# Fewer, larger transfers and a last row stored in seven pieces, in a kernel that scales tokens by their two gate weights

## The chip, the cores and the metric

The kernel runs on one core of a Trainium2 chip. The metric is the device time of one execution in microseconds (us), taken several times; lower is better. Besides the times there is one profiled execution, with the busy spans of every engine, the packets of the DMA engines and what released each wait.

## The reference

Each of 16 x 1024 tokens has 512 float32 values and 8 router logits. The two largest probabilities of a token are scaled so that they sum to 1, and the token is written out twice, once with each weight (the smaller first).

```python
def reference(x, router_logits, k):
    ...
    probs = probs / np.sum(probs, axis=-1, keepdims=True)
    topk_indices = np.argsort(probs, axis=-1)[..., -k:]
    topk_probs = np.take_along_axis(probs, topk_indices, axis=-1)
    topk_probs = topk_probs / np.sum(topk_probs, axis=-1, keepdims=True)
    x_expanded = x[:, :, np.newaxis, :].repeat(k, axis=2)
    return (x_expanded * topk_probs[..., np.newaxis]).astype(np.float32)
```

With k = 2 the weights are the two sigmoids of the difference of the two largest logits. The kernel reads 33.6 MB of x and 0.5 MB of logits and writes 67.1 MB.

## The kernel before

The 16,384 tokens are cut into two groups of 128 x 65 and 128 x 63 (`GROUPS`, L49). Within a group each of the 128 partitions holds 65 (or 63) consecutive tokens, here called rows: "16 rows" is 16 tokens on every partition. A row is 2 KB per partition in x and 4 KB per partition in the output, since each token is written twice. The core's on-chip memory holds one group of x in `xs` (65 rows), which is used again for the second group, and a staging buffer `osp` for 16 output rows.

*Weights.* After the first two loads (L114) both parts of the logits are loaded (L116, L117), and `top2_weights` finds the largest and second largest of 8 for all 128 tokens of a partition in ten small VectorE steps, their difference (L40), and two sigmoids on ScalarE (L42, L43). The result `WA` serves both groups.

*Rows.* A plan says which rows are multiplied in one VectorE instruction (L128) and where the products go; one store follows each (L136). There are two kinds of places: `osp`, and the part of `xs` whose tokens have already been read (`over`, L98 to L104): as 16 input rows become 32 rows' worth of output, a later stretch of rows can be written over earlier ones of `xs`. For each group the plan is: rows 0 and 1 to `osp`; rows 2 to 15 to `osp`; rows 16 to 31 over the first 32 rows of `xs`; rows 32 to 39 and 40 to 47 to the two halves of `osp`; then the rest (`LAST`, L54) over `xs`, in two parts of 9 and 8 rows in group 0 and one of 15 in group 1. Before a place is written again, the store that reads it must have landed: the multiply for rows 32 to 39 waits for the store of rows 2 to 15, and the loads of the second group wait for the stores out of `xs`.

*Queues.* All loads and stores are issued by SyncE, in program order, except the stores of two rows (L135), which are issued by ScalarE. A wait at one SyncE issue holds back everything behind it on SyncE. Group 1's loads stand in program order behind group 0's stores. The 16 DMA engines serve both queues.

Of the kernel before, what the change touches and what calls it, by code (L numbers as in the profile page):

```python
# [1 line left out]

# [4 lines left out]

F32 = mybir.dt.float32
ALU = mybir.AluOpType
ACTF = mybir.ActivationFunctionType  # L10
P = 128


def top2_weights(nc, pool, logits, M, E, tag=""):

    hi, lo, n = None, None, E  # L20
    while n > 1:
        n //= 2
        if hi is None:
            a, b = logits[:, :, 0:n], logits[:, :, n : 2 * n]
            nhi = pool.tile([P, M, n], F32, tag=f"hi{n}{tag}")
            nlo = b
            nc.vector.tensor_tensor(nhi, a, b, op=ALU.max)  # L27
            nc.vector.tensor_tensor(nlo, a, b, op=ALU.min)  # L28
        else:
            a, b = hi[:, :, 0:n], hi[:, :, n : 2 * n]  # L30
            nhi = pool.tile([P, M, n], F32, tag=f"hi{n}{tag}")
            nlo = pool.tile([P, M, n], F32, tag=f"lo{n}{tag}")
            tmp = pool.tile([P, M, n], F32, tag=f"tmp{n}{tag}")
            nc.vector.tensor_tensor(tmp, lo[:, :, 0:n], lo[:, :, n : 2 * n], op=ALU.max)  # L34
            nc.vector.tensor_tensor(nlo, a, b, op=ALU.min)  # L35
            nc.vector.tensor_tensor(nlo, nlo, tmp, op=ALU.max)  # L36
            nc.vector.tensor_tensor(nhi, a, b, op=ALU.max)  # L37
        hi, lo = nhi, nlo
    dlt = pool.tile([P, M], F32, tag=f"dlt{tag}")
    nc.vector.tensor_tensor(dlt, hi[:, :, 0], lo[:, :, 0], op=ALU.subtract)  # L40
    WA = pool.tile([P, M, 2], F32, tag=f"WA{tag}")
    nc.scalar.activation(WA[:, :, 0], dlt, ACTF.Sigmoid, scale=-1.0)  # L42
    nc.scalar.activation(WA[:, :, 1], dlt, ACTF.Sigmoid, scale=1.0)  # L43
    return WA

GROUPS = [65, 63]  # L49

LOADS = [[2, 4, 2, 8, 17, 32], [16, 16, 31]]


LAST = [[(48, 9), (57, 8)], [(48, 15)]]  # L54


@with_exitstack
def kernel(
    ctx: ExitStack,
    tc: tile.TileContext,  # L60
    x: bass.AP,
    router_logits: bass.AP,
    k: bass.AP,
    out: bass.AP,
):
    nc = tc.nc
    B, S, D = x.shape
    E = router_logits.shape[-1]
    N = B * S
    assert int(k) == 2 and E == 8 and N == P * sum(GROUPS)  # L70
    M = N // P

    L = 16
    x_v, o_v, rl_v = [], [], []
    t0 = 0
    for n in GROUPS:
        t1 = t0 + P * n
        x_v.append(
            x.rearrange("b s d -> (b s) d")[t0:t1].rearrange("(p m) d -> p m d", p=P)
        )  # L80
        o_v.append(
            out.rearrange("b s k d -> (b s) k d")[t0:t1].rearrange(
                "(p m) k d -> p m k d", p=P
            )
        )
        rl_v.append(
            router_logits.rearrange("b s e -> (b s) e")[t0:t1].rearrange(
                "(p m) e -> p m e", p=P
            )
        )  # L90
        t0 = t1

    wpool = ctx.enter_context(tc.tile_pool(name="wpool", bufs=1))
    logits = wpool.tile([P, M, E], F32)
    xs = wpool.tile([P, max(GROUPS), D], F32)
    osp = wpool.tile([P, L, 2, D], F32)

    def over(r, n, G):  # L98

        a = 2 * r - G
        return xs[:, a : a + 2 * n, :].rearrange("p (r k) d -> p r k d", k=2)  # L104

    h = L // 2
    e = 2
    m0 = 0
    for g, G in enumerate(GROUPS):
        r = 0  # L110
        for n in LOADS[g]:
            nc.sync.dma_start(xs[:, r : r + n, :], x_v[g][:, r : r + n, :])  # L112
            r += n
            if g == 0 and r == 6:  # L114

                nc.sync.dma_start(logits[:, :G], rl_v[0])  # L116
                nc.sync.dma_start(logits[:, G:], rl_v[1])  # L117
                WA = top2_weights(nc, wpool, logits, M, E)
        assert r == G
        begin = [(0, e, osp[:, :e]), (e, L - e, osp[:, e:])]  # L120
        plan = begin + [
            (L, L, over(L, L, 2 * L)),
            (2 * L, h, osp[:, :h]),
            (2 * L + h, h, osp[:, h:]),
        ]
        plan += [(r, n, over(r, n, G)) for r, n in LAST[g]]
        for r, n, og in plan:
            nc.vector.tensor_tensor(  # L128
                og,
                xs[:, r : r + n, :].unsqueeze(2).to_broadcast([P, n, 2, D]),  # L130
                WA[:, m0 + r : m0 + r + n, :].unsqueeze(3).to_broadcast([P, n, 2, D]),
                op=ALU.mult,
            )

            queue = nc.scalar if n == e else nc.sync  # L135
            queue.dma_start(o_v[g][:, r : r + n], og)  # L136
        m0 += G


# [1 line left out]
_INS = ['x', 'router_logits', 'k']  # L141
_OUTS = [((16, 1024, 2, 512), 'float32')]

_NUMBERS = {'k': 2}


# [26 lines left out]
```

## Time and profile before

| | |
|---|---|
| times of three runs | 241.50, 240.71, 241.03 us (median 241.03) |
| profiled execution, span from first to last instruction | 239.1 us |
| VectorE busy | 142.1 us, 24 instructions |
| of this, multiplies into `osp` (L128) | 69.2 us, 8 instructions |
| of this, multiplies into `xs` (L128) | 69.1 us, 5 instructions |
| ScalarE busy | 1.8 us |
| moved by DMA | 101.19 MB in 3,456 packets |

How to read the profile: "L128" is line 128 of the kernel. `out<-in` names what an instruction writes and reads. "SPq" and "ACTq" are the issuing sides of SyncE and ScalarE, on which a DMA is handed over; q1 is SyncE's DMA queue and q10 ScalarE's. A DMA's "landing" is the moment its last part is reported as arrived. A packet is counted in the stretch of time in which it starts, so in short stretches the shares of the DMA engines can pass 1. The windows view gives, for a stretch of time, the busy time of VectorE, ScalarE and GpSimd with the number of instructions, then the clock, the share of the DMA engines and GB/s.

### The profile page before, as it was taken

The numbers are of one execution on the slowest core, as the hardware profiler recorded it, in microseconds if no ns is written. First come the engines' busy times: TensorE is split into PE (matmuls) and PEld (weight loads), VectorE is DVE, ScalarE is ACT, GpSimd is POOL, SyncE is SP. The second block draws the span as 40 slices with busy tenths as digits, with TensorE's granted clock in tenths as the row PEclk, the third lists the DMA queues.
The fourth block names the chain that finished last, engine by engine and source line by source line (L and its number), as shares of the span: only waits on it lengthen the run. The fifth ranks groups of instructions, "written<-read, shape, count | busy, mean of one in ns | idle before, by whom it ended". The sixth has DMA issues, their size and how long they took to land.

```text
span 239.1 us, 118 instructions
## 1 busy us (share of the span) xinstructions
DVE 142.1 (59%) x24; ACT 1.8 (1%) x3; POOL 0.2 (0%) x4
## 2 busy tenths in 40 slices
DVE  0589999900299699900000699999006999990000
ACT  2000000000000000000000000000000000000000
POOL 0000000000000000000000000000000000000000
DMA  7999989899999999999999999899899898999894
GB/s 254 440 463 426 441 388 526 329 460 460 417 438 406 400 422 438 438 481 396 433 438 438 438 511 396 384 502 394 384 460 515 362 493 367 428 433 486 380 483 175
DMA packets 3456, 101.19 MB, mean 423 GB/s; under 512 B 384, under 2 KB 512, under 8 KB 896
## 3 DMA queue, kind: packets, MB, share of 16 engines
q1 hardware_dynamic: 3168, 99.09, 96.5%
q10 hardware_dynamic: 288, 2.10, 2.1%
HBM read 34.08 MB, written 67.11 MB: 423 GB/s over the span
## 4 chain that ended last, share of the span: by engine, by line
DMA 52%; DVE 33%; issue 4%; SPq 1%; ACT 0%; DVEq 0%
DMA out_dram<-xs 24%; DVE xs L128 18%; DVE osp L128 13%; DMA out_dram<-osp 13%; DMA xs<-in_x_dram 13%; DMA logits<-in_router_logits_dram 3%; SPq L112 0%; DVE nhi L27 0%; DVE logits L28 0%; DVE nlo L36 0%; DVE nhi L37 0%; DVE nlo L35 0%; DVE tmp L34 0%; SPq L116 0%; ACT WA L42 0%
## 5 line engine op out<-in xcount | busy, mean ns | idle before, releaser
L128 DVE TENSOR_TENSOR osp<-xs,WA 128x8192 f32<-128x8192 f32 (+2 forms) x8 | 69.2, 8688 | 62.3 <-DMA xs<-in_x_dram 31.2
L128 DVE TENSOR_TENSOR xs<-xs,WA 128x16384 f32<-128x16384 f32 (+3 forms) x5 | 69.1, 13811 | 2.2 <-DMA out_dram<-xs 2.0
L27 DVE TENSOR_TENSOR nhi<-logits 128x512 f32<-128x512 f32 x1 | 0.7, 691 | 8.5 <-DMA logits<-in_router_logits_dram 8.5
L42 ACT ACT_TABLE_LOAD x1 | 1.3, 1283 | 0.7 <-PEq L154 0.7
L28 DVE TENSOR_TENSOR logits<-logits 128x512 f32<-128x512 f32 x1 | 0.7, 691 | 0.0
L35 DVE TENSOR_TENSOR nlo<-nhi 128x256 f32<-128x256 f32 (+1 forms) x2 | 0.7, 351 | 0.0
L37 DVE TENSOR_TENSOR nhi<-nhi 128x256 f32<-128x256 f32 (+1 forms) x2 | 0.7, 351 | 0.0
L36 DVE TENSOR_TENSOR nlo<-nlo,tmp 128x256 f32<-128x256 f32 (+1 forms) x2 | 0.7, 350 | 0.0
L34 DVE TENSOR_TENSOR tmp<-logits 128x256 f32<-128x256 f32 x1 | 0.4, 417 | 0.0
L42 ACT ACTIVATE WA<-dlt 128x128 f32<-128x128 f32 x1 | 0.3, 315 | 10.4 <-DVE dlt L40 10.4
L40 DVE TENSOR_TENSOR dlt<-nhi,nlo 128x128 f32<-128x128 f32 x1 | 0.3, 291 | 0.0
L43 ACT ACTIVATE WA<-dlt 128x128 f32<-128x128 f32 x1 | 0.3, 298 | 0.0
L34 DVE TENSOR_TENSOR tmp<-nlo 128x128 f32<-128x128 f32 x1 | 0.3, 283 | 0.0
L154 POOL MEMSET const-bfloat16-1.0<- 128x1 bf16 x1 | 0.1, 101 | 0.0
L154 POOL MEMSET const-uint8-127<- 128x1 uint8 x1 | 0.1, 101 | 0.0
L154 POOL MEMSET const-float32-0.0<- 128x1 f32 x1 | 0.1, 98 | 0.2 <-issue 0.2
L154 POOL MEMSET const-float32-1.0<- 128x1 f32 x1 | 0.1, 98 | 0.0
## 6 DMA issues: line engine op xcount, KB each, us to landing
out_dram<-osp SPq DMA_DIRECT2D x4, 4096.0 KB, 20.7
out_dram<-osp SPq DMA_DIRECT2D x2, 7168.0 KB, 32.4
xs<-in_x_dram SPq DMA_DIRECT2D x2, 4096.0 KB, 30.4
xs<-in_x_dram SPq DMA_DIRECT2D x1, 7936.0 KB, 40.9
out_dram<-xs SPq DMA_DIRECT2D x1, 7680.0 KB, 23.1
out_dram<-xs SPq DMA_DIRECT2D x1, 4608.0 KB, 20.4
xs<-in_x_dram SPq DMA_DIRECT2D x1, 4352.0 KB, 22.8
out_dram<-xs SPq DMA_DIRECT2D x1, 4096.0 KB, 21.4
```

Of the source, the lines that this page charges most:

```text
L27: nc.vector.tensor_tensor(nhi, a, b, op=ALU.max)
L28: nc.vector.tensor_tensor(nlo, a, b, op=ALU.min)
L34: nc.vector.tensor_tensor(tmp, lo[:, :, 0:n], lo[:, :, n : 2 * n], op=ALU.max)
L35: nc.vector.tensor_tensor(nlo, a, b, op=ALU.min)
L36: nc.vector.tensor_tensor(nlo, nlo, tmp, op=ALU.max)
L37: nc.vector.tensor_tensor(nhi, a, b, op=ALU.max)
L40: nc.vector.tensor_tensor(dlt, hi[:, :, 0], lo[:, :, 0], op=ALU.subtract)
L42: nc.scalar.activation(WA[:, :, 0], dlt, ACTF.Sigmoid, scale=-1.0)
L43: nc.scalar.activation(WA[:, :, 1], dlt, ACTF.Sigmoid, scale=1.0)
L128: nc.vector.tensor_tensor(og, xs[:, r : r + n, :].unsqueeze(2).to_broadcast([P, n, 2, D]), WA[:, m0 + r : m0 + r + n, :].unsqueeze(3).to_b ...
L154: nc = _bacc.Bacc("TRN2", target_bir_lowering=False, num_devices=1)
```

## The change

The loads of group 0 are cut 6, 28 and 31 rows instead of 2, 4, 2, 8, 17 and 32; the logits are loaded behind the first of them. Group 1's loads stay 16, 16 and 31. The stores stand in a table, `STORES`, as (first row, rows, place): a number is a row of `osp`, `None` is over `xs`. In group 0 they have 2, 15, 16, 16 and 16 rows, in group 1 16, 16, 16 and 15. Only the first has 2 rows (`EARLY`) and goes to ScalarE's queue. `osp` has 18 rows instead of 16; the logits and the intermediate values of `top2_weights` now lie in its last three rows rather than in tiles of their own; the ten VectorE steps and two sigmoids are the same.

The very last row of group 1 (row 62 of each partition) is taken out of the last store, which then has 14 rows, and is stored in seven transfers of 60, 28, 13, 12, 8, 4 and 3 partitions, all issued by SyncE. That makes 17 whole transfers and 7 pieces instead of 24 whole transfers.

```diff
-LOADS = [[2, 4, 2, 8, 17, 32], [16, 16, 31]]
+LOADS = [[6, 28, 31], [16, 16, 31]]
-LAST = [[(48, 9), (57, 8)], [(48, 15)]]
+STORES = [
+    [(0, 2, 0), (2, 15, 2), (17, 16, None), (33, 16, 0), (49, 16, None)],
+    [(0, 16, 0), (16, 16, None), (32, 16, 0), (48, 15, None)],
+]
+EARLY = 2
+
+LAST_ROW = [[], [60, 28, 13, 12, 8, 4, 3]]
+OSP = 18
...
+    logits = osp[:, OSP - 1].rearrange("p k d -> p (k d)").rearrange("p (m e) -> p m e", e=E)
+    scratch = osp[:, OSP - 3 : OSP - 1].rearrange("p r k d -> p (r k d)")
...
         for n in LOADS[g]:
             nc.sync.dma_start(xs[:, r : r + n, :], x_v[g][:, r : r + n, :])
+            if g == 0 and r == 0:
+                nc.sync.dma_start(logits[:, : GROUPS[0]], rl_v[0])
+                nc.sync.dma_start(logits[:, GROUPS[0] :], rl_v[1])
+                top2_weights(nc, scratch, logits, WA)
             r += n
...
+        for r, n, home in STORES[g]:
+            if home is None:
+                a = 2 * r - (r + n)
+                og = xs[:, a : a + 2 * n, :].rearrange("p (r k) d -> p r k d", k=2)
+            else:
+                og = osp[:, home : home + n]
...
-            queue = nc.scalar if n == e else nc.sync
-            queue.dma_start(o_v[g][:, r : r + n], og)
+            queue = nc.scalar if n == EARLY else nc.sync
+            split = LAST_ROW[g] if r + n == G else []
+            whole = n - bool(split)
+            queue.dma_start(o_v[g][:, r : r + whole], og[:, :whole])
+            p0 = 0
+            for np_ in split:
+                queue.dma_start(
+                    o_v[g][p0 : p0 + np_, r + whole : r + n], og[p0 : p0 + np_, whole:]
+                )
+                p0 += np_
```

More of the change, by code (lines that the diff above doesn't have):

```diff
@@ L11, with top2_weights, cut @@
 P = 128
-def top2_weights(nc, pool, logits, M, E, tag=""):
-    hi, lo, n = None, None, E
+E = 8
+D = 512
+GROUPS = [65, 63]
+M = sum(GROUPS)
+LOADS = [[6, 28, 31], [16, 16, 31]]
[6 more added lines that the diff above has]
+OSP = 18
+def top2_weights(nc, scratch, logits, WA):
+    used = [0]
+    def cut(n):
+        a = scratch[:, used[0] : used[0] + M * n].rearrange("p (m n) -> p m n", n=n)
+        used[0] += M * n
+        return a
+    a, b = logits[:, :, 0:4], logits[:, :, 4:8]
+    hi = cut(4)
+    lo = b
+    nc.vector.tensor_tensor(hi, a, b, op=ALU.max)
+    nc.vector.tensor_tensor(lo, a, b, op=ALU.min)
+    n = 4
@@ L21, in top2_weights @@
     while n > 1:
         n //= 2
[L23 to L37, printed above, removed]
@@ L38, in top2_weights @@
-        hi, lo = nhi, nlo
[L39 to L49, printed above, removed]
-LOADS = [[2, 4, 2, 8, 17, 32], [16, 16, 31]]
-LAST = [[(48, 9), (57, 8)], [(48, 15)]]
+        a, b = hi[:, :, 0:n], hi[:, :, n : 2 * n]
@@ new lines, in top2_weights @@
+        nhi, nlo, tmp = cut(n), cut(n), cut(n)
+        nc.vector.tensor_tensor(tmp, lo[:, :, 0:n], lo[:, :, n : 2 * n], op=ALU.max)
+        nc.vector.tensor_tensor(nlo, a, b, op=ALU.min)
+        nc.vector.tensor_tensor(nlo, nlo, tmp, op=ALU.max)
+        nc.vector.tensor_tensor(nhi, a, b, op=ALU.max)
+        hi, lo = nhi, nlo
+    dlt = cut(1)
+    nc.vector.tensor_tensor(dlt, hi, lo, op=ALU.subtract)
+    nc.scalar.activation(WA[:, :, 0], dlt[:, :, 0], ACTF.Sigmoid, scale=-1.0)
+    nc.scalar.activation(WA[:, :, 1], dlt[:, :, 0], ACTF.Sigmoid, scale=1.0)
@@ L66 @@
     nc = tc.nc
[L67 to L73, printed above, removed]
+    N = x.shape[0] * x.shape[1]
+    assert int(k) == 2 and router_logits.shape[-1] == E and x.shape[2] == D
+    assert N == P * M
+    xf = x.rearrange("b s d -> (b s) d")
+    of = out.rearrange("b s k d -> (b s) k d")
+    rf = router_logits.rearrange("b s e -> (b s) e")
     x_v, o_v, rl_v = [], [], []
@@ L77 @@
         t1 = t0 + P * n
[L78 to L90, printed above, removed]
-        t0 = t1
[L93 to L107, printed above, removed]
+        x_v.append(xf[t0:t1].rearrange("(p m) d -> p m d", p=P))
+        o_v.append(of[t0:t1].rearrange("(p m) k d -> p m k d", p=P))
+        rl_v.append(rf[t0:t1].rearrange("(p m) e -> p m e", p=P))
+        t0 = t1
+    pool = ctx.enter_context(tc.tile_pool(name="pool", bufs=1))
+    xs = pool.tile([P, max(GROUPS), D], F32)
+    osp = pool.tile([P, OSP, 2, D], F32)
+    WA = pool.tile([P, M, 2], F32)
+    logits = osp[:, OSP - 1].rearrange("p k d -> p (k d)").rearrange("p (m e) -> p m e", e=E)
+    scratch = osp[:, OSP - 3 : OSP - 1].rearrange("p r k d -> p (r k d)")
     m0 = 0
@@ L112 @@
             nc.sync.dma_start(xs[:, r : r + n, :], x_v[g][:, r : r + n, :])
+            if g == 0 and r == 0:
+                nc.sync.dma_start(logits[:, : GROUPS[0]], rl_v[0])
+                nc.sync.dma_start(logits[:, GROUPS[0] :], rl_v[1])
+                top2_weights(nc, scratch, logits, WA)
             r += n
[L114 to L127, printed above, removed]
+        for r, n, home in STORES[g]:
[4 more added lines that the diff above has]
+                og = osp[:, home : home + n]
             nc.vector.tensor_tensor(
```

## Prediction

> **What bounds the kernel now.** I read the page first: engine shares, the strip of 40 slices, the DMA queues.
>
> ```profile
> span 239.1 us, 118 instructions
> DVE 142.1 (59%) x24; ACT 1.8 (1%) x3; POOL 0.2 (0%) x4
> DMA  7999989899999999999999999899899898999894
> q1 hardware_dynamic: 3168, 99.09, 96.5%
> q10 hardware_dynamic: 288, 2.10, 2.1%
> HBM read 34.08 MB, written 67.11 MB: 423 GB/s over the span
> ```
>
> VectorE works 59% of the span; the two DMA queues together occupy the 16 DMA engines for 98.6% of it, which is 235.7 us. So the bytes set the time, and the change leaves the bytes alone (101.19 MB). Next the windows view, to see whether any slack lies in the middle.
>
> ```profile
> 2.00:2.50 0.50, 0.00 (x0) 0.01 (x1) 0.00 (x0) 1.00 0.50 74
> 50.00:130.00 80.00, 35.74 (x4) 0.00 (x0) 0.00 (x0) 1.00 1.01 435
> 2.00:237.00 235.00, 142.05 (x24) 0.53 (x3) 0.00 (x0) 1.00 1.00 430
> ```
>
> (Columns: stretch, length, busy VectorE, ScalarE, GpSimd, clock, DMA share, GB/s.) From 2 to 237 us the share is 1.00, so there is no hole to close there, although the chain of waits walks through VectorE. The best steady rate is 435 GB/s. At that rate the bytes need 101.19/0.435 = 232.6 us; 239.1 minus 232.6 leaves 6.5 us for the start, transfer overheads, the mixed load and store stretches and the end. Only from these can this change gain.
>
> The end is seen in the DMA view, by counting packets that start in narrow stretches: 236.66 to 237.30, then to 237.95, then to 238.00. Each DMA engine closes a transfer with one tiny record, so a record tells when an engine is through.
>
> ```profile
> DMA packets 15, 0.00 MB, mean 0 GB/s; under 512 B 15, under 2 KB 15, under 8 KB 15
> DMA packets 0, 0.00 MB, mean 0 GB/s; under 512 B 0, under 2 KB 0, under 8 KB 0
> DMA packets 1, 0.00 MB, mean 0 GB/s; under 512 B 1, under 2 KB 1, under 8 KB 1
> ```
>
> Fifteen engines are through by 237.3; one comes 0.7 to 1.3 us behind them and alone sets the end. Taking the fifteen in the middle of their stretch, the mean is (15 x 236.97 + 237.97)/16 = 237.03, so perfect balance is worth 0.94 us.
>
> **The change part by part.** *Fewer transfers.* 24 whole transfers become 17. What one costs is seen in the DMA view over two stretches of equal bytes: 63.1 to 82.4 (one store of 16 rows), 82.4 to 101.75 (two of 8 rows), and, for small packets, 8.0 to 8.55.
>
> ```profile
> q1 hardware_dynamic: 144, 8.39, 100.3%
> q1 hardware_dynamic: 288, 8.39, 100.4%
> q1 hardware_dynamic: 55, 0.23, 99.4%
> ```
>
> 16-row store: 19.30 x 1.003 = 19.36 us per engine; two 8-row stores: 19.35 x 1.004 = 19.43. Splitting costs 0.07 us, overlap of packets taken out about 0.05. Seven fewer: 7 x 0.05 = 0.35 us gained. The seven pieces give some back: a 4 KB packet takes 0.55 x 16 x 0.994/55 = 0.159 us, where 4 KB inside the 64 KB packets take 19.36/8/16 = 0.151; 8 rows x 0.008 = 0.06, plus seven closing records, under 0.1. Net gain 0.2, bounds 0 to 0.4.
>
> *The second early store goes.* The old kernel puts rows 0 and 1 of each group on ScalarE's queue; the new one does so in the first group only (no store of the second has 2 rows). How late the late engine is, before and after that second early store, from the records in 122.36 to 122.85, to 123.20, to 123.24; then 179.87 to 180.50, to 181.15, to 181.20:
>
> ```profile
> DMA packets 30, 0.49 MB, mean 1003 GB/s; under 512 B 15, under 2 KB 15, under 8 KB 15
> DMA packets 0, 0.00 MB, mean 0 GB/s; under 512 B 0, under 2 KB 0, under 8 KB 0
> DMA packets 2, 0.03 MB, mean 819 GB/s; under 512 B 1, under 2 KB 1, under 8 KB 1
> DMA packets 30, 0.98 MB, mean 1560 GB/s; under 512 B 15, under 2 KB 15, under 8 KB 15
> DMA packets 0, 0.00 MB, mean 0 GB/s; under 512 B 0, under 2 KB 0, under 8 KB 0
> DMA packets 2, 0.07 MB, mean 1311 GB/s; under 512 B 1, under 2 KB 1, under 8 KB 1
> ```
>
> Distance from first to last: 123.2 - 122.36 = 0.84 before, 181.15 - 179.87 = 1.28 after, and the same 1.3 at the end. So 0.45 us of lateness came in where two queues interleaved. I take all 0.45 as gained; the lower bound is 0, if the lateness comes from elsewhere.
>
> *The last row.* Until now each engine gets 8 packets of each transfer (144 records = 128 packets + 16 closings). How rows of a 60- or 13-partition piece are shared out no row shows. Pieces of 13, 12, 8, 4 and 3 rows cannot reach all 16 engines, so some engines get fewer than 8 packets and others more. If the late engine gets none, it saves 8 x 0.159 = 1.27 us, and another, given perhaps three more (0.48), sets the end; if it is one of the favoured, it loses 0.48. Together with the previous item the gain cannot pass the 0.94 of perfect balance. I take 0.85 for both, 0.40 of it here, as the sizes fall so steeply that they fit one engine that is left out; range of both -0.48 to 0.94.
>
> The Trainium skill ("DMA: Bandwidth & Descriptors", section "Why a DMA increments its semaphore by 16 and not by 1") says that a transfer uses the largest divisor of its partition count up to 16, on the lowest-numbered engines. By it the sixteen engines would get 11, 11, 11, 10, 9, 9, 9, 9, 8, 8, 8, 8, 7, 6, 4 and 0 rows; no row of this profile numbers the engines.
>
> *Longer waits for the staging buffer.* `osp` now holds 16 rows per refill at rows 33 of group 0 and 32 of group 1, where the old code refilled it in two halves. The multiply must wait for the landing of the store before last, and its own store must be issued before the running one ends.
>
> ```profile
> 30.33 17.23 DVE L128 TENSOR_TENSOR xs<-xs,WA 128x16384 f32<-128x16384 f32 x1
> 47.58 0.34 SPq L136 DMA_DIRECT2D out_dram<-xs  x1
> 64.42 17.29 DVE L128 TENSOR_TENSOR osp<-xs,WA 128x8192 f32<-128x8192 f32 x2 [16.87 <-DMA out_dram<-osp]
> 73.14 8.93 SPq L136 DMA_DIRECT2D out_dram<-osp  x2
> 83.64 0.03 issue
> 83.74 9.77 DVE xs L128
> 0.73 0.86 SPq L112 DMA_DIRECT2D xs<-in_x_dram  x2
> ```
>
> (Timeline and chain; start, length.) Waking takes 0.10 (83.64 to 83.74), the 16-row multiply 17.24, SyncE's turn 0.02: the new store is issued 17.36 us after the landing. The store that runs meanwhile is 16 rows; landings around one lie 83.64 - 64.32 = 19.32 apart, and this landing at 83.64 comes 0.35 behind the late engine's closing record, which the DMA view has between 83.28 and 83.31:
>
> ```profile
> DMA packets 2, 0.03 MB, mean 1092 GB/s; under 512 B 1, under 2 KB 1, under 8 KB 1
> ```
>
> The late engine therefore runs dry 19.32 - 0.35 = 18.97 after the landing, the first ones 0.85 sooner, 18.1. What counts is the delay from issue to first packet. Nearest rows: the first load is issued at 0.73, and the DMA view has 17 packets starting in 1.74 to 2.20, so about 1.0; the other bound is ScalarE's first store, issued at 15.32, with only the other queue's packets until 18.78 and its own from there to 20.40.
>
> ```profile
> DMA packets 17, 0.07 MB, mean 151 GB/s; under 512 B 0, under 2 KB 0, under 8 KB 17
> 15.32 0.38 ACTq L136 DMA_DIRECT2D out_dram<-osp  x1
> q1 hardware_dynamic: 38, 1.32, 88.8%
> q10 hardware_dynamic: 17, 0.14, 20.3%
> ```
>
> That is 3.46 us, but behind packets of another queue already begun. I take 1.0: first packet at 17.36 + 1.0 = 18.36, so the first engines idle 0.26 and the late one not at all. Cost of the end: 0. At 3.46 the two places cost 2 x (3.46 - 1.61) = 3.7 us.
>
> *The start and the issue queue.* Logits now follow one 6-row load instead of 2 + 4: same bytes ahead, one issue less; the ten small VectorE steps stay. But the 15-row multiply waits for a 28-row load. Until that lands 8.9 MB of x, 0.5 of logits and up to 1.05 of early store move: at 435 GB/s, from about 2.3 us on, it lands at 24 to 26.5.
>
> ```profile
> L128 DVE TENSOR_TENSOR xs<-xs,WA 128x15360 f32<-128x15360 f32 x1 | 16.2, 16158 | 0.0
> L128 DVE TENSOR_TENSOR xs<-xs,WA 128x16384 f32<-128x16384 f32 x2 | 34.4, 17224 | 0.1
> SPq L112 <- DMA out_dram<-xs: 19.8, 2, 10.4
> 102.67 21.33 SPq L112 DMA_DIRECT2D xs<-in_x_dram  x3
> 215.19 0.33 SPq L136 DMA_DIRECT2D out_dram<-xs  x1
> ```
>
> With 16.16 us of multiply its store is issued at 40 to 43; all loads and the early store (18.6 MB) keep the engines until 45. Hidden, with 2 us to spare less the 1.0 of issue; without the cover, up to 1 us. The next 16-row multiply ends 17.2 later, at 60, while the 15-row store runs until 63: hidden too. In group 1 the third load still waits on SyncE for the landing of a store over `xs` (now near 122), and everything behind it on SyncE waits with it; two 16-row loads of 9.7 us each are then queued, and the next store is due only near 149. The seven piece issues come after the last multiply, near 213: 7 x 0.33 = 2.3 us of SyncE, hidden under 17 us of the store ahead of them.
>
> *Sum.* 0.2 + 0.45 + 0.40 = 1.05 us. Profiled span 239.1 - 1.05 = 238.05; the median of the runs, 241.03, lies 1.9 above that span, so **240.0 us**.
>
> **The rivals.** *The engines run dry at the two refills* (the slower side). For it: the margin is 18.97 - 18.36 = 0.6 us, where the old code had ten; ScalarE's delay of 3.46. Against: SyncE's ring is a single queue, and 1.0 was seen on it. It decides once the delay passes 1.61 + 1.05/2 = 2.1; at 2.85, midway from that to the far row, the price is 2 x 1.24 = 2.5, so 242.5 us, at most 243.7.
>
> *The pieces are slow.* Every store in this trace spans all 128 partitions, each engine with rows of its own. If engines that read neighbouring partitions hold each other up, a 60-row piece (4 packets an engine) and a 28-row piece (2) go at half pace, 1.27 + 0.64, and in the others up to four packets queue: 4 x 0.64 + 0.48. Against 11 x 0.159 = 1.75 that is 3.2 us more; half of it, as the engines are not in step, gives 240.0 + 1.6 = 241.6. For it: nothing in this trace; against it: nothing either. The Trainium skill ("SBUF — State Buffer", section on the DMA port swizzle) states the rule that speaks for it: partitions 0 to 63 reach only 8 of 16 ports, with 196 GB/s against 328 for all.
>
> *The change does not touch the late engine*: its lateness is not tied to the second queue, and the pieces do not spare it. Then only 0.2 is left: 240.8 us.
>
> **How the numbers follow.** Forecast 50%, dry engines 18%, slow pieces 20%, late engine untouched 12%. A measurement of this kernel can tell about 0.3%, 0.72 us: faster is below 240.31, slower above 241.75. The forecast's own range is 239.3 to 240.6 (0.94 + 0.4 gained, or half the sum lost); some 85% of it is faster, 43%, and 2% from the third rival: 0.45. Slower: 18% and half of the slow pieces: 0.28. The rest, 0.27, is no change. The range takes in the slow pieces and the lower part of the dry engines: 239.2 to 242.3.
>
> **What would show it.** Right: in the last microseconds the closing records of the row stores no longer leave one engine alone behind; the DMA share stays at 1.00 near 83 and 198 us; no early packets of the second queue in group 1; a span near 238. Wrong: slices below full DMA share right after the two 16-row `osp` multiplies (dry engines); 4 KB packets longer than 0.159 us in the last 3 us (slow pieces); one record 0.8 us behind the rest (late engine untouched). A hole near 43 us would mean that the 28-row load is too large.

## The result and the profile after

The changed kernel takes 243.72 us (median of 4 runs, 243.07 to 244.71) against 240.87 us for the kernel before, measured with it: a ratio of 1.0126, 95% interval 1.0089 to 1.0163. It is 2.85 us slower. The forecast was 240.0 us with a range of 239.2 to 242.3.

The page of the changed kernel, the lines that answer to those of before (below `DMA`, the rate in each of the 40 slices):

```profile
span 241.7 us, 108 instructions
DVE 141.8 (59%) x20; ACT 1.8 (1%) x3; POOL 0.2 (0%) x4
DMA  6998999999999989898979999998989898989993
GB/s 263 539 456 347 401 421 485 382 437 488 391 466 401 466 347 521 347 521 347 521 309 434 434 485 399 483 352 369 499 369 499 380 488 358 510 358 477 446 446 106
q1 hardware_dynamic: 2501, 100.14, 97.3%
q10 hardware_dynamic: 144, 1.05, 1.0%
```

VectorE is unchanged and the DMA engines are as busy as before: 98.3% of a span that is 2.6 us longer, for the same bytes. That is 237.6 us of packets per engine where it was 235.7, so some 1.9 of the 2.6 us is time in which packets were under way but took longer; the rest is idle time. The windows view says where (columns as in the prediction):

```profile
118.00:126.00 8.00, 0.00 (x0) 0.00 (x0) 0.00 (x0) 1.00 0.85 319
158.00:166.00 8.00, 8.00 (x1) 0.00 (x0) 0.00 (x0) 1.00 1.01 389
237.40:238.40 1.00, 0.00 (x0) 0.00 (x0) 0.00 (x0) 1.00 0.98 225
238.40:239.40 1.00, 0.00 (x0) 0.00 (x0) 0.00 (x0) 1.00 0.68 213
239.40:240.40 1.00, 0.00 (x0) 0.00 (x0) 0.00 (x0) 1.00 0.23 82
```

The same two stretches in the kernel before:

```profile
118.00:126.00 8.00, 0.00 (x0) 0.00 (x0) 0.00 (x0) 1.00 0.93 401
158.00:166.00 8.00, 8.00 (x1) 0.00 (x0) 0.00 (x0) 1.00 1.11 476
```

Three places, then. Near 120 us the engines turn from group 0's last store to group 1's first load; near 160 us they turn from group 1's last load to its first store. There the changed kernel is slower, though packets are counted whole in the stretch where they start, so a rate over 8 us is only a pointer. And at the end the pieces run at half the steady rate while the engines are 98% busy in the first of the three stretches.

For the turns I count packets instead. A stretch in which exactly the last 16 packets of a transfer start, one on each engine, gives their mean length: the share times the length of the stretch. The changed kernel in 119.75 to 120.40 (64 KB packets of the last store) and 158.75 to 159.75 (62 KB packets of the last load):

```profile
q1 hardware_dynamic: 16, 1.05, 483.2%
q1 hardware_dynamic: 16, 1.02, 323.9%
```

The kernel before at the same two turns, in 121.10 to 122.05 (32 KB) and 160.50 to 161.50 (62 KB):

```profile
q1 hardware_dynamic: 16, 0.52, 127.7%
q1 hardware_dynamic: 16, 1.02, 246.5%
```

After: 4.832 x 0.65 = 3.14 us against 2.42 for a 64 KB packet in the steady stretch, and 3.24 us. Before: 1.277 x 0.95 = 1.21 us, which is half of 2.42, and 2.47. For 62 KB the share of 2.42 is 2.34. So in the changed kernel these last packets are too long by 0.7 us at the first turn and 0.9 at the second, on average over the engines; the kernel before lost nothing at the first turn and 0.1 at the second. Below, such a lengthening is called a stall.

The refill that I expected to be tight, group 0's, is seen in the timeline of the changed kernel, and in its DMA view for 83.000 to 83.385 and 83.385 to 83.600:

```profile
65.30 17.23 DVE L112 TENSOR_TENSOR osp<-xs,WA 128x16384 f32<-128x16384 f32 x1 [5.69 <-DMA out_dram<-osp]
82.55 0.33 SPq L121 DMA_DIRECT2D out_dram<-osp  x1
```

```profile
DMA packets 5, 0.00 MB, mean 0 GB/s; under 512 B 5, under 2 KB 5, under 8 KB 5
DMA packets 14, 0.59 MB, mean 2743 GB/s; under 512 B 5, under 2 KB 5, under 8 KB 5
```

Up to 83.385 only closing records start; then nine first packets of the new store at once. The first packet comes 0.84 us after the issue. Five engines were done by 83.385 and idled, for 0.3 us at most, as worked out. At this place next to nothing was lost. What it led to later was not in the forecast.

Group 1's refill is another matter. In the profile of the changed kernel with its last row left whole (an experiment below), the new store is issued only at 201.20, and the DMA view for 200.10 to 200.90 and 202.02 to 202.20 shows fifteen closing records and one last packet of the running store, then fifteen first packets of the new one, with nothing starting in between:

```profile
201.20 0.33 SPq L121 DMA_DIRECT2D out_dram<-osp  x1
DMA packets 16, 0.07 MB, mean 82 GB/s; under 512 B 15, under 2 KB 15, under 8 KB 15
DMA packets 15, 0.98 MB, mean 5461 GB/s; under 512 B 0, under 2 KB 0, under 8 KB 0
```

So fifteen engines stood dry for more than 1.1 us. The refill had waited for the landing of an earlier store, and the sixteenth engine was a whole packet behind there; it closes the running store at 202.81 and goes straight on. In the changed kernel itself the gap at this place is shorter: thirteen engines close between 200.45 and 200.98, and the next packets start from 200.98 on.

### The profile page after: what moved, and what is told of

Read it like the earlier page. It is cut to its first block, busy times and chain, and to the rows that moved or that the text cites. A ratio compares the mean times of both kernels' runs of the same rounds, so it can differ in the third digit from the quotient of the medians.

```text
span 241.7 us, 108 instructions
## 1 busy us (share of the span) xinstructions
DVE 141.8 (59%) x20; ACT 1.8 (1%) x3; POOL 0.2 (0%) x4
## 3 DMA queue, kind: packets, MB, share of 16 engines
q10 hardware_dynamic: 144, 1.05, 1.0%
## 4 chain that ended last, share of the span: by engine, by line
DMA 46%; DVE 42%; SPq 1%; issue 0%; DVEq 0%
DVE osp L112 28%; DMA xs<-in_x_dram 24%; DMA out_dram<-osp 22%; DVE xs L112 14%; SPq L102 0%; SPq L103 0%; SPq L100 0%; SPq L121 0%; DVEq L112 0%
## 5 line engine op out<-in xcount | busy, mean ns | idle before, releaser
L112 DVE TENSOR_TENSOR osp<-xs,WA 128x16384 f32<-128x16384 f32 (+2 forms) x5 | 70.1, 14026 | 66.3 <-DMA xs<-in_x_dram 45.7
L112 DVE TENSOR_TENSOR xs<-xs,WA 128x16384 f32<-128x16384 f32 (+1 forms) x4 | 67.8, 16958 | 0.1
L45 DVE TENSOR_TENSOR osp<-osp 128x512 f32<-128x512 f32 x1 | 0.7, 693 | 8.0 <-DMA osp<-in_router_logits_dram 8.0
L46 DVE TENSOR_TENSOR osp<-osp 128x512 f32<-128x512 f32 x1 | 0.7, 693 | 0.0
L55 DVE TENSOR_TENSOR osp<-osp 128x256 f32<-128x256 f32 (+1 forms) x2 | 0.7, 354 | 0.0
L54 DVE TENSOR_TENSOR osp<-osp 128x256 f32<-128x256 f32 (+1 forms) x2 | 0.7, 354 | 0.0
L53 DVE TENSOR_TENSOR osp<-osp 128x256 f32<-128x256 f32 (+1 forms) x2 | 0.7, 353 | 0.0
L52 DVE TENSOR_TENSOR osp<-osp 128x256 f32<-128x256 f32 (+1 forms) x2 | 0.7, 353 | 0.0
L59 ACT ACTIVATE WA<-osp 128x128 f32<-128x128 f32 x1 | 0.3, 316 | 9.9 <-DVE osp L58 9.9
L60 ACT ACTIVATE WA<-osp 128x128 f32<-128x128 f32 x1 | 0.3, 300 | 0.0
```

What stands on the lines that cost most here:

```text
L45: nc.vector.tensor_tensor(hi, a, b, op=ALU.max)
L46: nc.vector.tensor_tensor(lo, a, b, op=ALU.min)
L59: nc.scalar.activation(WA[:, :, 0], dlt[:, :, 0], ACTF.Sigmoid, scale=-1.0)
L60: nc.scalar.activation(WA[:, :, 1], dlt[:, :, 0], ACTF.Sigmoid, scale=1.0)
L112: nc.vector.tensor_tensor(og, xs[:, r : r + n, :].unsqueeze(2).to_broadcast([P, n, 2, D]), WA[:, m0 + r : m0 + r + n, :].unsqueeze(3).to_b ...
```

## The experiments

Theory A is that the pieces are slow, B that they are not. For the stalls at the turns the theories came one after another; most fell. All ratios are against the kernel before on the same chip, and "us" is a median.

### The pieces

**The old kernel with the pieces, and the new one without.**

```diff
 # kernel before, group 1's last store
-            queue.dma_start(o_v[g][:, r : r + n], og)
+            split = [60, 28, 13, 12, 8, 4, 3] if g == 1 and r + n == G else []
+            whole = n - bool(split)
+            queue.dma_start(o_v[g][:, r : r + whole], og[:, :whole])
... (the loop over the pieces, as in the change)
 # changed kernel
-LAST_ROW = [[], [60, 28, 13, 12, 8, 4, 3]]
+LAST_ROW = [[], []]
```

> The kernel before, with only its very last row taken out and stored in the seven pieces. Theory A (pieces of fewer than 128 partitions are slow, because several DMA engines then read the same part of the on-chip memory): about 1.2 us slower than before, with 4 KB packets well above 0.159 us at the end. Rival B (the pieces balance the engines as forecast, and all of the loss lies in the middle): 0.4 to 0.9 us faster than before.

> The changed kernel, with the last row left in the last store of 15 rows. Theory A: 1.2 us faster than the changed kernel, so about 242.5 us, still 1.3 to 1.7 us slower than before, and the stalls near 120 and 159 us are still there. Rival B: slower than the changed kernel by 0.4 to 0.9 us, about 244.3.

Measured: the old kernel with pieces 240.90 us, ratio 1.0027 (1.0016 to 1.0038), 0.65 us slower. The new one with a whole last row 242.75 us, ratio 1.0083 (1.0057 to 1.0110), so 0.0043 or 1.0 us less than with pieces, though these two intervals overlap. The pieces lose 0.65 to 1 us; B falls. In the trace of the new kernel the DMA view from 237.37 to 240.50 us holds just the last row and closing records:

```profile
DMA packets 213, 0.52 MB, mean 168 GB/s; under 512 B 85, under 2 KB 85, under 8 KB 213
q1 hardware_dynamic: 213, 0.52, 60.7%
```

213 less 85 records gives the 128 rows. The share of 3.13 us on 16 engines is 30.4 us; less 85 x 0.009 for the records (the view of 16 records further below has 1.4% of 0.65 us), 29.6/128 = 0.23 us for a 4 KB packet instead of 0.159. And 85 is 16 + 69: one closing record per engine for the 14-row store, and 15 + 14 + 13 + 12 + 8 + 4 + 3 = 69 for the pieces. That is the number of engines that the Trainium skill ("DMA: Bandwidth & Descriptors", "Why a DMA increments its semaphore by 16 and not by 1") gives for these partition counts; the trace agrees.

**The disputed price by itself: one 16-row store in two halves of 64 partitions.**

```diff
+            if g == 1 and r == 16:
+                for p in (0, 64):
+                    queue.dma_start(o_v[g][p : p + 64, r : r + n], og[p : p + 64])
... (else the store as it was)
```

> The changed kernel with the last row left whole, and one 16-row store of group 1 (rows 16 to 31) cut into two transfers of 64 partitions each. If engines that read one half of the partitions share the ports that half has (theory A, at its strictest): the store takes twice as long, 19 us more in all, with its packets at 4.8 us instead of 2.42. If there is no such sharing: under 0.3 us more.

Measured: 261.43 us, ratio 1.0874 (1.0844 to 1.0905): 18.7 us above the 242.75 of the same kernel without the halves. Windows of this run, before, in the two halves, and after them:

```profile
165.00:180.00 15.00, 3.13 (x1) 0.00 (x0) 0.00 (x0) 1.00 0.98 424
182.00:198.00 16.00, 15.46 (x1) 0.00 (x0) 0.00 (x0) 1.00 0.96 201
200.00:214.00 14.00, 14.00 (x1) 0.00 (x0) 0.00 (x0) 1.00 0.91 187
220.00:234.00 14.00, 0.00 (x0) 0.00 (x0) 0.00 (x0) 1.00 0.97 421
```

Half the rate with the engines over 90% busy: no engine is left out, but each packet takes about twice as long. The rule of the Trainium skill ("SBUF — State Buffer", the DMA port swizzle) that was set against the change is borne out: 201 and 187 GB/s for these stores, 196 on its page for 64 partitions.

### The turns: what it is not

**Cut the store ahead of the turn.** Group 0's last 16 rows as two multiplies and two stores of 8 (new kernel, last row whole).

```diff
-    [(0, 2, 0), (2, 15, 2), (17, 16, None), (33, 16, 0), (49, 16, None)],
+    [(0, 2, 0), (2, 15, 2), (17, 16, None), (33, 16, 0), (49, 8, None), (57, 8, None)],
... (the place over `xs` is worked out so that the same rows of it are written)
```

> As the previous one, and the last store of group 0 is cut into two of 8 rows, so that 32 KB packets instead of 64 KB ones stand in front of group 1's loads. Theory C (a switch from stores to loads costs more behind large packets): the stall near 120 us goes, 0.5 to 1.0 us faster than the previous one. Rival D (those stalls come and go from run to run whatever the packets): no difference beyond the scatter, and stalls of 0.5 us or more still in the last packets of that store.

Measured: 242.90 us, ratio 1.0103 (1.0084 to 1.0122), no gain. Theory C falls: 32 KB packets stalled there too, with 1.95 us where the kernel before has 1.21 (the last 16 of them, 120.98 to 121.58).

**Four single edits of the old kernel.**

```diff
 # no second early store
+        begin = ... if g == 0 else [(0, L, osp)]
 # last store of group 0 in one
+LAST = [[(48, 17)], [(48, 15)]]
 # refill of 16 rows
-            (2 * L, h, osp[:, :h]),
-            (2 * L + h, h, osp[:, h:]),
+            (2 * L, L, osp),
 # three loads
+LOADS = [[6, 28, 31], [16, 16, 31]]
```

> The kernel before, with rows 0 to 15 of group 1 in one multiply and one store, so that the second small store on ScalarE's queue is gone. Theory E (that store, running between group 1's last load and its first large store, softens the switch from loads to stores): 0.7 to 1.2 us slower than before, with packets of that last load stalled by 0.5 us or more near 160 us. Rival (my forecast: the second queue is what makes one engine late): 0.2 to 0.5 us faster.

> The kernel before, with group 0's last 17 rows in one multiply and one store instead of 9 + 8. Theory F (the stall at the switch from stores to group 1's loads comes with this larger store, or with when the loads behind it are issued): 0.5 to 1.0 us slower, packets near 120 us stalled by 0.5 us or more. Rival (it comes from something else the change did, as the run that cut this store in two and kept its stall suggests): within 0.3 us of before.

> The kernel before, with rows 32 to 47 of both groups in one 16-row multiply and one store instead of two of 8. Theory G (the engines run dry behind the longer multiply; a delay from issue to first packet above 1.6 us would be needed to lose time): up to 1 us slower at each place. Forecast's step: no loss, within 0.3 us of before, with the first engines idle 0.3 us near 83 us.

> The kernel before, with group 0's loads cut 6, 28 and 31 rows. Forecast's step: hidden, 0 to 0.2 us faster. Rival H (the later first large store changes how loads and stores meet near 43 us): 0.3 to 1 us slower, seen as a hole or stalled packets near 43 us.

| edit of the old kernel | us | ratio (95%) |
|---|---|---|
| no second early store | 240.37 | 1.0011 (0.9998 to 1.0024) |
| one 17-row store at the end of group 0 | 242.20 | 1.0079 (1.0065 to 1.0093) |
| 16-row refill | 241.20 | 1.0037 (1.0024 to 1.0049) |
| three loads | 240.31 | 1.0002 (0.9993 to 1.0011) |

The loads and the early store do nothing, against theories E and H and against my 0.45 us. Two edits cost 1 and 2 us. In both a multiply became longer and a store larger, and both now stalled at the turn near 121 us: 1.67 us for a 32 KB packet with the 16-row refill, and 2.03 for one of 34 KB, whose share is 1.29, with the 17-row store (the last 16 packets, in 120.9 to 121.5 and 121.9 to 122.4). Theory F seemed right for one, but the cut store above had not helped.

**Size or lateness?** First the refill multiplied in one but stored in two (old kernel); then the new kernel's 16-row stores cut 8 + 8 and 15 + 1 with the multiplies left; then one load more, to move every later transfer by one place.

```diff
+            for c in [slice(0, h), slice(h, L)] if r == 2 * L else [slice(0, n)]:
+                queue.dma_start(o_v[g][:, r + c.start : r + c.stop], og[:, c])
...
+            for c in [slice(0, 8), slice(8, 16)] if n == 16 else [slice(0, n)]:
...
+LOADS = [[2, 4, 2, 8, 8, 9, 32], [16, 16, 31]]
```

> The kernel before with rows 32 to 47 in one 16-row multiply, as in the run that cost 1.0 us, but stored in two transfers of 8 rows. Theory I (transfers with 64 KB or more on a partition, of which there is one ahead of group 1's loads in the kernel before and two or more in every kernel that stalled, make the next switch from stores to loads stall): no stall near 121 us, within 0.3 us of before. Rival J (the later issue behind the long multiply does it): the 1.0 us stays, with stalled packets near 121 us.

> The changed kernel with the last row left whole and every 16-row store issued as two of 8 rows; multiplies and loads stay as changed. Theory I: the stalls near 120 and 159 us go, 2.0 to 2.5 us faster than with 16-row stores, about 240.3 us. Rival J (long multiplies and late issues): 242 us or more, stalls stay.

> The same with stores of 15 rows (60 KB on a partition) and 1 row. Theory I with the step at 64 KB: as fast as the 8-row stores within 0.5 us. If instead the size of the packets matters smoothly: most of the stalls stay, above 241.5 us.

> The kernel before with the 17-row load cut into 8 and 9, so that every later transfer stands one place further in SyncE's queue. Theory I: no change within 0.3 us. Rival K (what counts is the place of a transfer in the queue, the number of transfers ahead of group 1's first load): stalled packets near 121 us and 1 us or more slower.

Measured: 241.40 us, ratio 1.0047 (1.0028 to 1.0066), so the loss stays with 8-row stores; 243.15 us, 1.0115 (1.0082 to 1.0148); 241.72 us, 1.0071 (1.0045 to 1.0097); 240.28 us, 1.0002 (0.9986 to 1.0017). Theory I falls twice, K falls, and J, the late issue, is left. (The 15 + 1 stores are the best of the new kernel's variants with long refills, but its interval overlaps that of the whole stores; I draw nothing from it.)

### The turns: a store that is issued late

In the first of these runs everything from 93 us up to group 1's refill near 199 us, which lies behind both turns, is as in the old kernel: the same transfers, in the same order, of the same size, issued within half a us of the same times. Only one store had been issued at 81 instead of 73 us, when the engines had almost finished what was queued. SyncE's issues in this run, then the one of the old kernel that answers to the last:

```profile
81.21 0.81 SPq L136 DMA_DIRECT2D out_dram<-osp  x2
93.07 9.06 SPq L136 DMA_DIRECT2D out_dram<-xs  x2
93.52 9.06 SPq L136 DMA_DIRECT2D out_dram<-xs  x2
```

The last 16 packets before the turn, in 121.1 to 121.7 of the same run:

```profile
q1 hardware_dynamic: 16, 0.52, 292.4%
```

2.924 x 0.6 = 1.75 us instead of 1.21. That is about half of the loss. Most of the rest lies where group 1's small store meets the loads, the first turn from loads to stores in group 1: between 138.7 and 140.8 us, 31 load packets of 32 KB take 1.42 us on average, in the old kernel 1.21, which is another 0.4 us for each engine.

To take the long multiply out I delayed the same issue in another way: a multiply is done twice, 8 or 6 of its rows. VectorE is then late for the rest of group 0 too, so that the later issues of that group also move.

```diff
+            if g == 0 and r == 2 * L:
+                nc.vector.tensor_tensor(
+                    og[:, :8],
+                    xs[:, r : r + 8, :].unsqueeze(2).to_broadcast([P, 8, 2, D]),
+                    WA[:, m0 + r : m0 + r + 8, :].unsqueeze(3).to_broadcast([P, 8, 2, D]),
+                    op=ALU.mult,
+                )
```

> The kernel before, with the 8-row multiply of rows 32 to 39 done twice, so that its store is issued near 81.8 instead of 73.1 us: the same transfers in the same order, only late. Theory L (what costs is a store issued when the engines have under about 1 us of queued work left; nothing is lost there, but the next switches between loads and stores stall): stalled packets near 121 us, about 1.0 us slower than before, no hole near 82 us. Rival M (the long multiply or the larger transfers themselves): within 0.3 us of before.

> The same with only 6 of the 8 rows done twice, so that the store is issued near 79.7 us, 2.7 us ahead of the end of the running one. Theory L: between nothing and 1.0 us, which tells how much queued work is enough; a margin of 4.6 us, as in the run with three loads, lost nothing. Rival M: within 0.3 us of before.

Measured: 8 rows 241.23 us, ratio 1.0053 (1.0034 to 1.0073); 6 rows 240.12 us, 0.9999 (0.9991 to 1.0008). The timeline with 8 rows done twice, then with 6:

```profile
64.04 8.69 DVE L129 TENSOR_TENSOR osp<-xs,WA 128x8192 f32<-128x8192 f32 x1 [16.88 <-DMA out_dram<-osp]
81.37 8.93 SPq L143 DMA_DIRECT2D out_dram<-osp  x2
99.76 9.06 SPq L143 DMA_DIRECT2D out_dram<-xs  x2
```

```profile
64.01 6.56 DVE L129 TENSOR_TENSOR osp<-xs,WA 128x6144 f32<-128x6144 f32 x1 [16.71 <-DMA out_dram<-osp]
79.20 8.93 SPq L143 DMA_DIRECT2D out_dram<-osp  x2
97.59 9.06 SPq L143 DMA_DIRECT2D out_dram<-xs  x2
```

The running store ends at 82.4 on the first engine: in the DMA view of the kernel with 8 rows twice (its profiled execution took 242.54 us, above its median), 82.41 to 83.00 holds the 15 closing records and 16 first packets of the next store, so there is no hole.

```profile
DMA packets 31, 0.52 MB, mean 889 GB/s; under 512 B 15, under 2 KB 15, under 8 KB 15
```

Issued 1.0 us ahead of that moment, the store loses nothing there but 1 us later; issued 3.2 us ahead, nothing at all. The last 16 packets before the turn, in 121.1 to 121.7, first with 8 rows done twice, then with 6:

```profile
q1 hardware_dynamic: 16, 0.52, 300.8%
```

```profile
q1 hardware_dynamic: 16, 0.52, 202.2%
```

3.008 x 0.6 = 1.80 us against 2.022 x 0.6 = 1.21. A delay of 2.2 us in the issues of group 0, with the engines busy throughout, makes the turn 40 us later stall, with no longer multiply and no larger transfer. Theory L holds for this place, M falls. This pair does not say which of the late issues counts, as later ones come close too: the second of the two stores is issued 2.1 us ahead of the end of the queue with 8 rows and 4.3 with 6, the next one 2.0 and 4.2. In the run before, one late store alone was enough. The runs at this place and at the end of group 0, in one table (the issue from the timeline; the end of what is queued is the first closing record of the transfer ahead, from the DMA view):

| kernel | issue | end of what is queued | ahead by | cost |
|---|---|---|---|---|
| before | 73.1 | 82.4 | 9.3 us | none |
| old, 6 rows twice | 79.2 | 82.4 | 3.2 us | none |
| old, 16-row refill | 81.1 | 82.3 | 1.2 us | 1.0 us |
| old, 8 rows twice | 81.4 | 82.4 | 1.0 us | 1.0 us |
| old, 17-row last store | 101.7 | 101.8 | 0.1 us | 2.0 us |

The last row is another case: there the engines do run dry. All sixteen close the store ahead within 101.70 to 102.50, and the first packets start within 102.50 to 102.80, 0.9 us after the issue:

```profile
DMA packets 16, 0.00 MB, mean 0 GB/s; under 512 B 16, under 2 KB 16, under 8 KB 16
DMA packets 16, 0.56 MB, mean 1857 GB/s; under 512 B 0, under 2 KB 0, under 8 KB 0
```

So part of its 2.0 us is this hole, some 0.3 to 0.8 us on an engine, and only the rest is the stall.

**Back to the changed kernel: refills halved, then row 49 halved as well** (last row whole).

```diff
+    [(0, 2, 0), (2, 15, 2), (17, 16, None), (33, 8, 0), (41, 8, 8), (49, 16, None)],
+    [(0, 16, 0), (16, 16, None), (32, 8, 0), (40, 8, 8), (48, 15, None)],
```

> The changed kernel with the last row left whole, and both 16-row refills of the staging buffer cut back into 8 + 8 rows. Theory L: most of the stalls near 120 and 159 us go, 240.2 to 241.2 us; the 16-row store at row 49 still has only 3 us of queued work ahead of it. Rival M: the 16-row store at row 49 stays, so 242 us or more.

> The same with group 0's last 16 rows cut into 8 + 8 as well, so that no issue comes with less than about 3 us of queued work ahead. Theory L: as fast as before or up to 0.4 us faster, no stalls near 120 us. Rival M: faster than the previous one by the whole of what is left.

Measured: 240.91 us, ratio 1.0035 (1.0022 to 1.0049), and 240.97 us, 1.0033 (1.0021 to 1.0046). Halving the refills takes back 1.0083 - 1.0035 = 0.0048, or 1.2 us; halving row 49 nothing, where theory L had expected the time of the kernel before. 0.7 us was left, most of it as stalled packets at the second turn. There, in 157.6 to 159.0 of the first of the two (its profiled execution took 242.08 us, above its median):

```profile
q1 hardware_dynamic: 16, 1.02, 211.4%
```

2.114 x 1.4 = 2.96 us for a 62 KB packet, whose share of 2.42 is 2.34. In the second, whose profiled execution took 240.94 us, it is 2.92 (158.1 to 159.0). The edit halves both refills, so the two places are not told apart.

**The last 0.7 us.** The old kernel with both harmless edits, and the changed kernel above with its 28-row load cut into 11 and 17, so that the first large multiply starts at 14.9 instead of 26.1 us.

```diff
 # old kernel: three loads and no second early store
+LOADS = [[6, 28, 31], [16, 16, 31]]
...
 # new kernel, refills and row 49 halved
-LOADS = [[6, 28, 31], [16, 16, 31]]
+LOADS = [[6, 11, 17, 31], [16, 16, 31]]
```

> The kernel before with both edits that cost nothing alone: three loads in group 0 and no second small store in group 1 (19 transfers instead of 24). If the 0.7 us left in the run with halved refills comes from these two together: 240.7 to 241.1 us and stalled packets near 160 us. If not: within 0.3 us of before; a gain of more than 0.3 us would show the 0.2 us that my forecast gave to fewer transfers and more.

> The changed kernel with whole last row, halved refills and halved row 49, and with the 28-row load cut into 11 and 17, so that the 15-row multiply starts some 10 us earlier and its store and the next come with far more queued work ahead. Theory L, if 3.3 us of queued work is still too little in front of that store: the last 0.7 us go, 240.2 us or less. Otherwise no change from 240.9 us.

Measured: 240.29 us, ratio 1.0005 (0.9996 to 1.0014), so it isn't the combination; and 240.34 us, 1.0002 (0.9990 to 1.0013), so the start of group 0 it is. The issues of the first two large stores without the cut load, then with it:

```profile
42.30 0.35 SPq L121 DMA_DIRECT2D out_dram<-osp  x1
59.56 0.34 SPq L121 DMA_DIRECT2D out_dram<-xs  x1
```

```profile
31.04 0.35 SPq L121 DMA_DIRECT2D out_dram<-osp  x1
48.30 0.34 SPq L121 DMA_DIRECT2D out_dram<-xs  x1
```

and the last 16 packets before the second turn in the latter, 158.0 to 158.6:

```profile
q1 hardware_dynamic: 16, 1.02, 402.3%
```

2.41 us: the stall is gone. No version beat the kernel before by anything that can be measured.

## Why the prediction was wrong, point by point

**Fewer transfers, 0.2 us: not found.** The old kernel with 20 transfers instead of 24 (nine loads became six and one store went; the expectation above counts 19) stands at 1.0005 (0.9996 to 1.0014). The 0.05 us of packet time saved per transfer is real in the trace, but the gain, if there is one, is below what these runs resolve.

**The second early store, 0.45 us: wrong.** Without it the old kernel is at 1.0011 (0.9998 to 1.0024). The step took one engine's 1.3 us from one execution for a property of the kernel. In another execution with that store kept (the old kernel with three loads), all 16 closing records start within 236.50 to 237.15:

```profile
DMA packets 16, 0.00 MB, mean 0 GB/s; under 512 B 16, under 2 KB 16, under 8 KB 16
```

And the median that the forecast started from was 241.03, where later runs of the same kernel had medians of 240.1 to 240.3. The 0.94 us of "perfect balance" were largely not there to be won.

**The last row, 0.40 us gained: wrong in sign.** It loses 0.65 us in the old kernel. The rival "slow pieces" had the mechanism right, and the price that it gave over the forecast, 1.6 us, stands against 0.4 + 0.65 = 1.05 or 0.4 + 1.0 = 1.4 us found. Whether an engine left out would have helped hardly matters beside that.

**Longer waits for the staging buffer, "cost of the end: 0": the step that failed.** At group 0's refill its arithmetic held: issue to first packet 0.84 us where I took 1.0, first engines idle about 0.3 us, late one not at all. The rival "dry engines" put its price on a hole at the refill and its decision at a delay of 2.1 us; here no such hole came. What both missed is that an issue this close to the end of the queue is paid for at the next turn between stores and loads. At group 1's refill engines did run dry, for more than 1.1 us on fifteen of them with the last row whole, but not for the rival's reason: the delay from issue to first packet was 0.83 us there too. The sum took the late engine as 0.85 us behind the first; after the turns, in that profile, it was 2.7 us behind the first, and the refill waits for the last. What that hole adds to the time is not shown, since the engine that was behind never waited. Taking both refills back is worth 1.2 us in the changed kernel, the largest term.

**The start of group 0, "hidden": right for the place, wrong for the whole.** No hole came near 43 us, but the changed kernel pays 0.0033 - 0.0002 = 0.0031, 0.75 us, for the late first stores. The old kernel with the same three loads pays nothing, with its first large store issued at 41.2 and the second at 58.5, about 1.1 us earlier than here.

**The sum.** 0.0043 for the pieces, 0.0048 for the refills and 0.0031 for the start make 0.0122 of the measured 0.0126. The parts come from single kernels taken back one after another, so that they add up is a consistency, not a proof that they are independent: in the old kernel a late issue at one place costs 1 us, at another, with a hole, 2. Two bounds beside the sum were miscounted, without effect on the outcome: the forecast's own range would start at 241.03 - 0.94 - 0.4 = 239.7, not 239.3, and midway between 2.1 and 3.46 lies 2.8, not 2.85.

**What stays open.** Why a late issue is paid 40 us later is not shown; the packets tell where the time goes and not why. Nor is there one number for enough work: 3.2 us ahead of a 64 KB store was enough, while 3.4 us ahead in group 0's loads and 4.2 at the next store went with the 0.7 us. That the first or the second of these two issues is the one that counts was not tried apart.

## What to carry to other kernels

In a kernel bound by its transfers, judge a longer compute step by how much queued work is left when its store is issued, not only by whether the engines run dry there: here 1 us left was too little, some 4.6 us and more was safe everywhere. Splitting the last row by partitions to balance the DMA engines lost 0.65 to 1 us here, and a store that covers only one half of the partitions ran at half the rate. And a lag of one engine in a single profiled execution has to be seen in a second one before it is worth a term.

## What the runs showed of the hardware

A store of 64 neighbouring partitions ran at 187 to 201 GB/s against 424 for 128 partitions, with the DMA engines over 90% busy.

The issues of the seven pieces took 8.53 us on SyncE, 1.2 us each, where a whole store takes 0.33. I had counted 0.33. It was hidden behind the store ahead. That the small number of partitions does it is not shown: in the same trace the issues of two whole loads of group 1, one right behind the other, took 1.2 us each too, and the longest of all the loads' issues is 1207 ns. The last whole store and the pieces in the timeline, and the loads by their line:

```profile
216.38 0.33 SPq L121 DMA_DIRECT2D out_dram<-xs  x1
216.75 8.53 SPq L124 DMA_DIRECT2D out_dram<-xs  x7
L100 SPq DMA_DIRECT2D xs<-in_x_dram x6: 328/486/1207, 0.7 to 123.8; - x6
```

And the turn between stores and loads was free or cost an engine 0.5 us or more on average, depending on how late a store was issued 40 us before: 1.21 us for the last 32 KB packets in the kernel before, 1.75 with one store issued 8 us later.
